# Moving a step's piece of attention ahead of its item of weight preparation in a two-layer fp32 block

## The chip, the core and the metric

The kernel runs on one core of one Trainium2 chip. The metric is the device time of one execution in microseconds (us). An execution of the kernel before takes 744.51 us, the median of three runs (743.21, 744.51 and 744.68).

## What is computed

The reference is a block of two equal layers. Sixteen learned meta tokens are put ahead of 512 input tokens, so T = 528, with a model width D of 1024, all in fp32. One layer does this:

```
h    = rms_norm(x, norm_gain)
proj = h @ w_in                      # q, k, v, gate_a, u_b, gate_b, q_idx, k_idx, w_idx, merge
q, k = rope(rms_norm(q)), rope(rms_norm(k));  q_idx, k_idx = rope(q_idx), rope(k_idx)
score[t, s] = sum over 8 heads of relu(q_idx . k_idx) * w_idx      # indexer
sel  = top 128 keys by score, in key chunks of 64 up to the query's own
attn = softmax(q . k over sel) @ v            # 8 heads of 64, one shared k and v
y_a  = (attn * silu(gate_a)) @ w_branch_a
y_b  = (pooled(u_b) * silu(gate_b)) @ w_branch_b
g_a, g_b = split(sigmoid(merge))              # 1024 columns each
x    = x + (g_a * y_a + g_b * y_b) @ w_out
```

The result is x after the two layers, without the meta tokens' rows.

## The kernel before

**Engines and orders.** TensorE (PE) and VectorE (DVE) run in the order in which the program issues their instructions (L101, a manual schedule for these two). ScalarE (ACT), GpSimd (POOL) and the DMA queue of SyncE (SP) are ordered by a scheduler, from the program's dependencies and from marks that the program sets. `Metered` (L52) adds up an estimated time for each instruction issued on PE and DVE; the program uses these sums to decide how much top-k selection it lets out.

**fp32 by halves.** A product of fp32 matrices is made of three matmuls on a faster type: high by high, low of the activations by high of the weights, high by low. For every weight there is a high part, a cast on ACT (L269), and a low part, a subtract on DVE of the high part from the raw weight. In the profile both are tiles named `w`, and DVE's instructions all carry line L63, that of the recording helper.

**Weight preparation.** Each chunk of 256 columns of `w_in` is multiplied by a scheme with seven products in place of eight, with the operands a11, a12, s2, s1, s3, s4 and a22. `mixed_prep` splits what a chunk needs into nine items, i0 to i8. An item is a few instructions: a cast of the next operand (`hi`), the subtract of the one before (`lo`), in some a sum on DVE (`s`, `raw<-s,raw`) and a DMA on POOL that adds one raw half to another (L255, L284). The last, i8, also issues the load of a later chunk on SP. The items wait in a queue, `prep_q`; `prep_one` takes the next. There are four raw buffers and eight `w` buffers.

**Groups of products.** `group_of_products` issues seven products of twelve matmuls each. `end()` follows every product: it calls `group_done`, and then takes further items until the chunk is as far ahead as `LEAD` (5 items) and the number of products done ask for. Copies of PSUM banks, `p` and `u` (ACT, L1019), and sums of a bank with such a copy, `c<-d,p` or `sila<-d,p` (DVE), set a bank free for a later product. `mix_gates` runs ten groups a layer; gates are tanh on ACT (L1059, L1065, L1069) and a multiply on DVE (`zb`, `sila`).

**Pieces of attention.** In `mix_gates` the attention is let out beside the products. Its generator makes three pieces a unit (a pair of heads of one block of 128 queries, sixteen units a layer): first the logits of the next unit on PE with the scaling of this one (reciprocal `rs` on DVE, `lt<-lt,rs` at L805 on ACT or on DVE, `pm` at L806 on POOL or DVE); then the softmax of the next unit (`lt<-a,sc` and `mn` on DVE, two exponentials at L791 on ACT) and the values of earlier ones on PE; then transposes on PE and their copies `pt` and `ptm` (ACT, L821 and L839), and the gated result `sila<-v,sila` (DVE). For the last four units the softmax comes with the first piece. `half_done` adds half of `rate` to a credit and lets out as many pieces as it has whole ones; `rate` is 1.4 and later 2.2 in the first layer, 1.6 in the second (L31). In the stage of the indexer, before these, `half_done` lets out indexer steps in the same way. An exponential is marked to be issued after the last copy of `p` or `u`.

**A step.** `group_done` does, in this order: instructions that became due (`later`), one item of preparation while `hold` allows one, `half_done`, and top-k selection as far as the metered time of PE leaves over.

Of the kernel before, what the change touches and what calls it, by code (L numbers as in the profile page):

```python
# [91 lines left out]
def tile_block(ctx: ExitStack, tc: tile.TileContext, x, meta, w_in, pool_w, w_a, w_b, w_out, rows, hgain, c_tab, out):  # L92
# [76 lines left out]
    def prep_one():  # L169
        popped[0] += 1  # L170
        prep_q.popleft()()
# [175 lines left out]
    def pump(n=1):  # L347
        for _ in range(n):
            while fill:
                try:  # L350
                    next(fill[0])
                    break
                except StopIteration:
                    fill.popleft()
# [6 lines left out]
    def half_done():  # L361
        credit[0] += rate[0] / 2
        n = int(credit[0])
        credit[0] -= n
        pump(n)

    def group_done():
        count[0] += 1
        due = [p for p in pend if p[0] <= count[0]]
        for p in due:  # L370
            pend.remove(p)
        for p in due:
            p[1]()
        if prep_q and hold[0]:
            hold[0] -= 1
            prep_one()
        half_done()
        spare[0] += share[0] * (pe.us - seen[0]) - (dve.us - seen[1])
        spare[0] = min(spare[0], CAP)
        seen[0], seen[1] = pe.us, dve.us  # L380
        while spare[0] > 0 and sel:
            before = dve.us
            try:
                next(sel[0])
            except StopIteration:
                sel.popleft()
            spare[0] -= dve.us - before
        seen[1] = dve.us
# [603 lines left out]
    def group_of_products(r, base, n2, operands, total, direct, mid=None):  # L992
# [18 lines left out]
        def end():  # L1011
            done[0] += 1
            group_done()
            while prep_q and (popped[0] < base + 9 * r + LEAD + done[0] * 9 // 7 or (mid and done[0] > 4)):
                prep_one()
# [202 lines left out]
    for l in range(2):  # L1218
# [20 lines left out]
        for t in (1, 2):  # L1239
            later(lambda t=t, ps=pss[t]: kv_post(l, t, ps), 1)  # L1240
        later(lambda ps=pss[0]: meta_sum(ps, KV, lambda total: kv_post(l, 0, total)), 1)
        group_done()
        for what, t in (("q", 1), ("q", 2), ("k", 3), ("k", 4), ("q", 3), ("q", 4)):
            if what == "k":
                ps = plain_group(t, raws[kv])
                later(lambda t=t, ps=ps: kv_post(l, t, ps), 1)
            else:
                index_queries(t, 0, w, hooks[1] if (l, t) == (1, 1) else None)
                if (l, t) == (0, 1):
                    ends.append(norm_half(0, 1, rstd, LAG1))  # L1250
            group_done()
            if (what, t) == ("k", 3):
                w_prep_enqueue(True, None if l else ends[0])
            if (what, t) == ("k", 4):
                del raws[kv]
                w_load()
# [318 lines left out]
```

## Time and profile before

| | us |
|---|---|
| median of the three runs | 744.51 |
| the profiled execution's own time | 744.49 |
| its span, first to last instruction | 742.7 |
| PE busy | 732.6 (99%) |
| weight loads of PE busy | 705.6 (95%) |
| DVE busy | 590.9 (80%) |
| ACT busy | 482.4 (65%) |
| POOL busy | 242.8 (33%) |

The granted clock of TensorE is 1.000. The merged-gate stages, in which attention runs beside the products, lie at about 172 to 310 us (first layer) and 538 to 664 us (second layer). A line of the timeline gives the start in us, the duration, the engine and line, the operation, the output and the inputs by the program's names, shapes, a count, and in brackets how long the engine had idled before and what released it. Lines of the waits view give the engine, what it was about to do, whom it waited for, and the total, the number and the longest of these waits.

### The profile page before, as it was taken

To read this page: it belongs to the slowest core of one execution; us is meant where nothing else is said; L and a number is where in the kernel's file an instruction comes from. 1 tells how busy PE (TensorE), PEld (TensorE's weight loads), DVE (VectorE), ACT (ScalarE), POOL (GpSimd) and SP (SyncE) were. 2 spreads that over 40 slices of the span, in tenths; PEclk is the share of its full clock that TensorE was granted. 3 is DMA by queue.
4 is the path that set the end of the run, shared out by engine and by line. 5 is a ranking of instruction groups with operands and counts; after the bars stand their busy time and mean duration, and the time that the engine had idled before them with its cause. 6 is when DMAs were issued, how large, how long until landed. Compare 5 with 4: busy or idle time off the path is not lost.

```text
span 742.7 us, 16105 instructions
## 1 busy us (share of the span) xinstructions
PE 732.6 (99%) x5949; PEld 705.6 (95%) x5949; DVE 590.9 (80%) x1500; ACT 482.4 (65%) x1099; POOL 242.8 (33%) x320
## 2 busy tenths in 40 slices
PE   8999999999999999999999999999999999999998
PEld 7999999899999999999999989998899999999997
DVE  6876899999897875894449668999989978768874
ACT  6669735656778886543236696367478977865643
POOL 3652173721221310063347410756021222105300
PEclk9999999999999999999999999999999999999999
DMA  8766774864564533543422677659464653448832
GB/s 265 231 154 165 166 158 114 214 158 100 119 139 114 123 64 101 173 156 117 143 88 86 170 171 198 157 128 204 109 156 100 147 111 86 116 107 261 201 89 72
DMA packets 103567, 106.42 MB, mean 143 GB/s; under 512 B 5008, under 2 KB 83632, under 8 KB 103488
## 3 DMA queue, kind: packets, MB, share of 16 engines
q1 hardware_dynamic: 91888, 74.89, 33.4%
q0 software_dynamic: 11520, 30.41, 22.8%
q8 instruction: 47, 0.77, 0.4%
q14 instruction: 32, 0.26, 0.1%
q10 hardware_dynamic: 80, 0.08, 0.0%
HBM read 66.41 MB, written 8.55 MB: 101 GB/s over the span
## 4 chain that ended last, share of the span: by engine, by line
PE 65%; DVE 23%; ACT 5%; issue 2%; DMA 2%; POOL 2%; SPq 1%; DVEq 0%; POOLq 0%; ACTq 0%
PE d L63 52%; PE a L63 9%; DVE sc L63 6%; DVE m L63 4%; PE v L63 4%; DVE w L63 2%; DVE t L63 2%; DMA xt<-in_x_dram 2%; ACT lt L791 1%; DVE lt L63 1%; DVE silb L63 1%; DVE us L63 1%; DVE mlo L63 1%; ACT w L225 1%; DVE qs L63 1%
## 5 line engine op out<-in xcount | busy, mean ns | idle before, releaser
L63 PE MATMUL d<-hhi,w 128*128 128x256 f32 (+3 forms) x1392 | 278.6, 291 | 0.8 <-DVE c L63 0.7
L63 PEld LDWEIGHTS d<-hhi,w 128*128 128x128 f32 x1392 | 222.4, 188 | 3.9 <-DVE c L63 1.2
L63 PE MATMUL d<-hlo,w 128*128 128x256 f32 (+3 forms) x696 | 189.9, 289 | 0.0
L63 DVE TENSOR_TENSOR w<-raw,w 128x512 fp32r<-128x512 f32 (+1 forms) x156 | 121.7, 786 | 20.7 <-ACT w L269 20.3
L63 PEld LDWEIGHTS d<-hlo,w 128*128 128x128 f32 x696 | 131.3, 189 | 1.4 <-issue 0.2
L63 PE MATMUL d<-hsum,w 128*128 128x264 f32 (+1 forms) x720 | 95.9, 285 | 0.6 <-ACT u L1019 0.3
L63 PEld LDWEIGHTS d<-hsum,w 128*128 128x128 f32 x720 | 89.6, 188 | 1.7 <-ACT u L1019 0.8
L63 PE MATMUL d<-w,hhi 128*128 128x256 f32 x576 | 86.1, 287 | 0.7 <-ACT sq L668 0.7
L269 ACT CAST w<-raw 128x512 fp32r<-128x512 f32 x132 | 78.7, 621 | 3.3 <-DMA raw<-s 1.4
L63 PEld LDWEIGHTS d<-w,hhi 128*128 128x128 f32 x576 | 74.7, 188 | 5.2 <-issue 2.3
L255 POOL DMA_DIRECT2D raw<-raw x22 | 19.8, 902 | 114.6 <-DMA raw<-in_w_in_dram 42.8
L221 POOL DMA_DIRECT2D w<-raw x34 | 31.5, 943 | 73.8 <-ACT w L220 51.1
L63 DVE MATCH_REPLACE8 sc<-m,sc 128x400 f32<-128x400 f32 (+2 forms) x100 | 54.5, 549 | 0.0
L791 ACT ACTIVATE lt<-lt,mn,NR 128x144 f32<-128x144 f32 (+3 forms) x64 | 42.2, 661 | 18.2 <-DVE mn L63 18.0
L63 DVE MAX8 m<-sc 128x8 f32<-128x400 f32 (+2 forms) x100 | 53.2, 557 | 0.9
L284 POOL DMA_DIRECT2D raw<-s x22 | 19.3, 879 | 91.0 <-DVE s L63 32.7
L63 DVE SCALAR_TENSOR_TENSOR sc<-r,wsg,sc 128x144 f32<-128x144 f32 (+3 forms) x56 | 32.4, 582 | 17.3 <-ACT r L714 15.0
L63 PE MATMUL d<-w,hlo 128*128 128x256 f32 x288 | 45.5, 281 | 0.0
L63 PE MATMUL d<-mhi,w 128*128 128x272 f32 (+2 forms) x192 | 45.2, 324 | 0.0
L677 POOL TENSOR_TENSOR t<-t,t 128x256 f32<-128x256 f32 (+1 forms) x34 | 32.5, 955 | 26.4 <-DVE t L63 25.0
L1420 POOL TENSOR_TENSOR hlo<-ta,hhi 128x256 fp32r<-128x256 f32 (+1 forms) x28 | 26.8, 966 | 43.6 <-PE d L63 31.4
L806 POOL TENSOR_SCALAR pm<-lt,rs 128x16 f32<-128x16 f32 x48 | 24.6, 573 | 47.3 <-DVE rs L63 47.3
(245 smaller groups left out, 1560.0 us busy)
## 6 DMA issues: line engine op xcount, KB each, us to landing
raw<-in_w_in_dram SPq DMA_DIRECT2D x88, 256.0 KB, 3.5
w<-raw POOLq DMA_DIRECT2D x34, 512.0 KB, 5.9
raw<-in_w_in_dram SPq DMA_DIRECT2D x32, 512.0 KB, 4.4
raw<-in_w_out_dram SPq DMA_DIRECT2D x12, 512.0 KB, 3.8
raw<-raw POOLq DMA_DIRECT2D x22, 256.0 KB, 4.2
raw<-s POOLq DMA_DIRECT2D x22, 256.0 KB, 3.3
kept<-res SPq DMA_DIRECT2D x16, 264.0 KB, 4.1
res<-kept SPq DMA_DIRECT2D x16, 264.0 KB, 6.4
```

Of the source, the lines that this page charges most:

```text
L63: return fn(*a, **k)
L221: gp.dma_start(t, raws[c][s], accum_op=OP.add)
L225: act.copy(t, raws[c][s])
L255: gp.dma_start(raws[c][0][:, 1], raws[c][0][:, 0], accum_op=OP.add)
L269: act.copy(t[:, 0], blk[src[n]])
L284: gp.dma_start(blk["a12"], blk["s2"], accum_op=OP.add)
L677: added[0] = gp.tensor_tensor(t1[:m, :256], t1[:m, :256], t2[:m, :256], op=OP.add).ins
L791: act.activation(L[hh][:, :n], L[hh][:, :n], AF.Exp, scale=NR[:, i, h:h + 1], bias=mn[:, hh:hh + 1], accum_out=sm[:, hh:hh + 1])
L806: (gp if j < 3 else dve).tensor_scalar(pms[i][:, 2 * j + hh, :], L[hh][:, 0:16], rs[:, hh:hh + 1], None, op0=OP.mult)
L1420: pool_end = gp.tensor_sub(hlo[:, j, a:a + n], d, f(hhi[:, j, a:a + n]))
```

## The change

In `group_done` the call of `half_done` goes ahead of the item of preparation. So in each step the piece of attention (or indexer step), if the credit lets one out, is issued before the item, and the item after it. Top-k selection still comes last, and no other line is changed.

```diff
         for p in due:
             p[1]()
+        half_done()
         if prep_q and hold[0]:
             hold[0] -= 1
             prep_one()
-        half_done()
         spare[0] += share[0] * (pe.us - seen[0]) - (dve.us - seen[1])
         spare[0] = min(spare[0], CAP)
```

The items that `end()` takes after `group_done` stay where they were, and so do those that a product takes because it needs them at once.

## The prediction

> **What bounds the kernel now.** I read the page first: the busy rows and the chain that ended last.
>
> ```profile
> PE 732.6 (99%) x5949; PEld 705.6 (95%) x5949; DVE 590.9 (80%) x1500; ACT 482.4 (65%) x1099; POOL 242.8 (33%) x320
> PE 65%; DVE 23%; ACT 5%; issue 2%; DMA 2%; POOL 2%; SPq 1%; DVEq 0%; POOLq 0%; ACTq 0%
> ```
>
> TensorE (PE) is busy 99% of the span and has the same matmuls in the same order after the change. The time can fall only by PE's waits and rise only by new ones. Attention and preparation of weights share the group steps where the orders of the two builds differ, and those are the two stages of merged gates. I split each into a tight half and a loose half by the windows view (us; then PE, PEld, DVE, ACT, POOL busy with counts; clock; DMA share; GB/s).
>
> ```profile
> 172.00:212.00 40.00, 39.26 (x326) 38.72 (x326) 36.35 (x103) 30.82 (x84) 7.84 (x14) 1.00 0.53 119
> 212.00:310.00 98.00, 97.84 (x869) 95.08 (x866) 74.79 (x204) 76.16 (x182) 17.12 (x27) 1.00 0.45 107
> 538.00:600.00 62.00, 61.56 (x534) 60.20 (x533) 56.41 (x163) 52.11 (x137) 16.05 (x24) 1.00 0.56 128
> 600.00:664.00 64.00, 63.84 (x587) 62.27 (x587) 45.22 (x123) 48.87 (x113) 11.77 (x17) 1.00 0.44 104
> ```
>
> In 172 to 212 and 538 to 600 VectorE (DVE) is busy 91% and ScalarE (ACT) 77 to 84% of the time, so a queue position there counts; later DVE falls to 71 to 76%. The waits view of PE's weight loads gives the ceiling, first of layer 0 (172 to 310), then of layer 1 (538 to 664); the second fence has DVE's waits for the casts, a row for each stage (total, times, longest).
>
> ```profile
> PEld d L63 <- DVE c L63: 1.2, 2, 1.0
> PEld d L63 <- ACT p L1019: 0.3, 1, 0.3
> PEld a L63 <- ACT lt L805: 0.2, 1, 0.2
> ...
> PEld d L63 <- ACT u L1019: 0.8, 2, 0.5
> PEld a L63 <- ACT lt L805: 0.5, 3, 0.2
> PEld a L63 <- DVE lt L63: 0.4, 1, 0.4
> PEld d L63 <- DVE w L63: 0.2, 1, 0.2
> ```
>
> ```profile
> DVE w L63 <- ACT w L269: 7.8, 9, 2.4
> DVE w L63 <- ACT w L269: 12.2, 12, 2.0
> ```
>
> These waits add up to 1.7 us in layer 0 and 1.9 us in layer 1: 3.6 us in all. More than that the change cannot win by removing waits that the trace names.
>
> **The change, part by part.** Nothing is added and nothing removed. Per step one item of preparation (a cast on ACT, a subtract "low" on DVE, sometimes a sum or a DMA) goes behind one piece of attention. In the built order PE is identical, DVE differs in 554 lines, ACT in 365, POOL in 72, SP in 10; all the differences lie in the two merged stages. The budget of the top-k selection sees the same amount of DVE work, since both pieces still precede it. What one place is worth on DVE is the low:
>
> ```profile
> L63 DVE TENSOR_TENSOR w<-raw,w 128x512 fp32r<-128x512 f32 x57 | 39.0, 686 | 11.6 <-ACT w L269 11.4
> ```
>
> A piece moved ahead of one low comes 0.69 us sooner; a low pays with the piece's length, 0.16 us for a reciprocal, 0.74 for the smallest softmax lead (144 columns, 198.37 to 199.11 below), more for wider ones.
>
> *Gain 1, layer 0, at 204.57.* DVE, ACT and PE rows of the timeline:
>
> ```profile
> 197.77 0.69 DVE L63 TENSOR_TENSOR w<-raw,w 128x512 fp32r<-128x512 f32 x1
> 198.37 0.31 DVE L63 CUSTOM_DVE_ANT_0 lt<-a,sc 128x144 f32<-128x144 f32 x1
> 198.95 0.16 DVE L63 TENSOR_TENSOR mn<-mn,RQ 128x2 f32<-128x2 f32 x1
> 199.20 0.51 ACT L791 ACTIVATE lt<-lt,mn,NR 128x144 f32<-128x144 f32 x1 [1.78 <-DVE mn L63]
> 201.44 0.43 DVE L63 SCALAR_TENSOR_TENSOR zb<-c,zb 128x264 f32<-128x264 f32 x1 [0.84 <-ACT c L1065]
> 203.55 0.28 PE L63 MATMUL d<-hhi,w 128*128 128x264 f32 x1
> 204.10 0.41 DVE L63 TENSOR_TENSOR c<-d,p 128x264 f32<-128x264 f32 x1
> 204.57 0.39 PE L63 MATMUL d<-hhi,w 128*128 128x264 f32 x1 [0.74 <-DVE c L63]
> ```
>
> PE waits for the total that frees its bank. The chain back is total, zb (0.84 us of DVE idle), the tanh behind two exponentials on ACT, and these wait 1.78 us for mn. In the new order mn stands ahead of the low of 197.77, 0.69 us sooner, and the tanh also passes a cast; zb's idle time goes, and the total comes about 0.8 sooner. PE lost 204.57 - 203.55 less one spacing of 0.12 = 0.9 there. I take 0.8 (ends 0.6 and 0.9). Next late there is DVE itself.
>
> *Gain 2, layer 1, at 540.57.* The same with a bank copy:
>
> ```profile
> 538.98 0.16 DVE L63 TENSOR_TENSOR mn<-mn,RQ 128x2 f32<-128x2 f32 x1
> 539.17 0.51 ACT L791 ACTIVATE lt<-lt,mn,NR 128x144 f32<-128x144 f32 x1 [1.58 <-DVE mn L63]
> 540.17 0.35 ACT L1019 COPY u<-d 128x256 f32<-128x256 f32 x1
> 538.32 1.94 PE L63 MATMUL d<-hsum,w 128*128 128x256 f32 x15
> 540.57 0.63 PE L63 MATMUL d<-hsum,w 128*128 128x256 f32 x3 [0.31 <-ACT u L1019]
> ```
>
> The 15 matmuls are 0.119 apart, so the next was due at 540.10: 0.47 lost, since the copy starts only as the second exponential ends. With mn 0.69 sooner all 0.5 goes (ends 0.3 and 0.5).
>
> *Smaller gains*, each bounded by its row of the first waits fence and by nothing: the copy of p in layer 0 (0.3; its exponentials follow a softmax lead that now passes a low), scaled rows L805 (0.2 and 0.5, of which I take 0.2 and 0.4, because reciprocals go ahead of low and sum), and lt scaled on DVE in layer 1 (0.4, likewise). Gains together: 0.8 + 0.5 + 0.3 + 0.2 + 0.4 + 0.4 = 2.6 us. The second wait for u and the "DVE w" row I leave standing (0.5 us).
>
> *Give-back 1, layer 1, at 557.* A cast goes behind exponentials:
>
> ```profile
> 551.50 0.61 ACT L269 CAST w<-raw 128x512 fp32r<-128x512 f32 x1
> 552.01 0.51 ACT L791 ACTIVATE lt<-lt,mn,NR 128x144 f32<-128x144 f32 x1
> 552.15 0.69 DVE L63 TENSOR_TENSOR w<-raw,w 128x512 fp32r<-128x512 f32 x1 [0.88 <-ACT w L269]
> 555.92 0.69 DVE L63 TENSOR_TENSOR w<-raw,w 128x512 fp32r<-128x512 f32 x1
> 557.28 0.40 PE L63 MATMUL d<-hhi,w 128*128 128x256 f32 x2
> ```
>
> DVE, already waiting for that cast, waits two exponentials longer: 2 x 0.505 = 1.01 (551.50 and 552.01 swap places). Nothing makes it up before the low of 555.92, which also has a reciprocal (0.16) put before it. That low ends at 556.60; the third matmul of its product, at 557.28, is the first to use it, and a release takes about 0.05 (204.51 to 204.57 above), so 0.63 covers it: 1.01 + 0.16 - 0.63 = 0.54 lost. Ends: 0, if the gain before it carries over in full, and 1.2, if PE comes there sooner and DVE doesn't. By the Trainium skill ("ScalarE: Activation LUTs", What ACT_TABLE_LOAD costs) an ACTIVATE with a pointer as bias takes about 280 ns + 0.833 ns a column, 0.40 us at 144, and consecutive ones overlap by 0.09; two of them would then delay the cast by some 0.6, and this term would fall to 0.15 as an estimate, the sum to about -1.6. The trace has 0.51 from start to start, each with an accumulator read, and the trace decides.
>
> *Give-backs 2 to 5.* The copy of p at 208.17 gets two exponentials ahead of it:
>
> ```profile
> 208.17 0.38 ACT L1019 COPY p<-d 128x264 f32<-128x264 f32 x1
> 208.96 0.62 ACT L791 ACTIVATE lt<-lt,mn,NR 128x272 f32<-128x272 f32 x1
> 209.86 0.41 PE L63 MATMUL d<-hsum,w 128*128 128x264 f32 x2
> ```
>
> It moves by 2 x 0.61 = 1.22, ending at 208.55 + 1.22 = 209.77 against PE's 209.86: between 0 and 0.8, if PE arrives by gain 1 earlier and the copy doesn't. I take 0.2. Three lows (one early in layer 0's loose half, two in layer 1's tight half) pay a softmax lead or a gated product ahead of them, and are ready for PE with about as much to spare; I put each between 0 and the 0.54 of give-back 1, and take 0.2. Together 0.8.
>
> *What costs nothing.* In the loose halves lows move back by a reciprocal, a scaled row and a whole lead of 528 columns, about four times 0.74 = 3.0 us. There the weight is ready long before use:
>
> ```profile
> 633.76 0.69 DVE L63 TENSOR_TENSOR w<-raw,w 128x512 fp32r<-128x512 f32 x1 [1.37 <-ACT w L269]
> 639.00 0.40 PE L63 MATMUL d<-hhi,w 128*128 128x256 f32 x2
> ```
>
> That low ends at 634.45, its first use is the third matmul of a product, at 639.00: 4.5 us, of which 1.5 stay; where less is left, PE would pay the difference, under 1 us. On POOL a few meta products (L806) pass the DMAs that add raw halves, and the load on SP follows a low that is later, by at most that 3.0. DVE's two stages show no wait for these DMAs, so I count nothing; without that cover the late piece costs up to 3 us once. On SP a load of the residual passes two of w_out, which are used in the stage after: nothing.
>
> *Sum.* -2.6 + 0.54 + 0.8 = -1.26 us. The profiled execution took 744.49 (span 742.7, 1.8 around it), as good as the median 744.51. 744.49 - 1.26 = 743.2.
>
> **The rivals.**
> (a) *The gains without the give-backs*: the ring of DVE and ACT starts earlier and stays earlier, so no low is late: 744.49 - 2.6 = 741.9. For it: both large waits stand at the beginning of their stage. Against: the lows move back by design at every step. All 3.6 us gone would give 740.9.
> (b) *No change*: DVE is 91% busy in the tight halves, and what PE stops waiting for is replaced by the next low: gains 1.3, give-backs 1.3: 744.5.
> (c) *Slower: casts behind exponentials.* By the built orders sixteen casts in 172 to 212 and 538 to 590 go behind one or two exponentials (0.5 to 0.6 us each), and DVE waits for casts 21 times already (the two rows above, 20.0 us). If three more places lose 0.54 as at 557 and the gains halve, 744.49 - 1.3 + 1.34 + 3 x 0.54 = 746.2; with no gain left, 747.5. It decides once the give-backs pass 2.6 + 1.5 = 4.1 us at full gains, or 2.8 at half. Against it: before the change PE waits only 0.2 us for a low in the whole of layer 1's stage. The Trainium skill ("PSUM — Partial Sum Buffer", Engine vs sequencer instructions) speaks for it: it calls ACT's and DVE's queues strictly first in, first out, so nothing passes a waiting exponential. The trace agrees where the copy of u starts at 540.17, as the exponential of 539.17 and its twin end.
>
> **How the numbers follow.** Forecast 0.38, (a) 0.17, (b) 0.13, (c) 0.32. About 0.2% (1.5 us, below 743.0 or above 746.0) is what a measurement of this kernel tells from no change. The forecast's own range is 742.2 to 744.2, by the ends of its terms: half of it counts as faster. With (a) faster is 0.19 + 0.17 = 0.36; same has the rest of the forecast, (b) and the lowest part of (c), 0.19 + 0.13 + 0.03 = 0.35; slower the rest of (c), 0.29. The range reaches to (a) below and past the middle of (c) above: 741.6 to 746.9.
>
> **What the profile after would show.** Right: PE's wait for c at about 204 and for u at about 540 gone, exponentials' waits for mn shorter in the tight halves; DVE's waits for casts grown in 538 to 600, one PE wait for a low or a hole of about 0.5 near 557, the loose halves unchanged within 0.3 us. Wrong: several new PE waits for w or p in the tight halves (c), a DVE wait for a sum or load, or PE's waits for c and u still there, because ACT orders the tanh and copies otherwise than I read them.

## The result

The changed kernel takes 740.65 us (median of 6 runs, 740.39 to 742.35). The kernel before, run beside it, took 743.75 us over all its 6 runs (743.02 to 744.68), 0.76 us less than the median shown ahead of the prediction. The ratio is 0.9964 with a 95% interval of 0.9953 to 0.9974, so it is faster, by 3.1 us between the medians and by 0.36% by the ratio. The prediction of 743.2 us (741.6 to 746.9) missed it. Rival (a), 741.9 us with gains and no give-backs, came nearest.

The page of the profile after has this busy row, then the chain:

```profile
PE 731.2 (99%) x5949; PEld 705.3 (95%) x5949; DVE 590.0 (80%) x1500; ACT 483.1 (65%) x1099; POOL 246.1 (33%) x320
PE 75%; DVE 17%; ACT 2%; DMA 2%; issue 2%; POOL 1%; SPq 1%; DVEq 0%; POOLq 0%; ACTq 0%
```

The engines are busy for as long as before, within 4 us each; PE's share of the chain rose from 65% to 75%, those of DVE and ACT fell. The windows view of the four halves, with the columns of the prediction's:

```profile
172.00:212.00 40.00, 39.93 (x335) 39.39 (x335) 37.43 (x108) 31.69 (x85) 8.82 (x14) 1.00 0.57 132
212.00:310.00 98.00, 97.97 (x865) 95.31 (x863) 74.48 (x200) 76.24 (x180) 18.03 (x27) 1.00 0.46 109
538.00:600.00 62.00, 61.95 (x543) 61.13 (x542) 56.23 (x159) 52.60 (x137) 18.92 (x26) 1.00 0.58 133
600.00:664.00 64.00, 64.00 (x591) 62.78 (x590) 46.01 (x123) 49.13 (x112) 9.93 (x15) 1.00 0.44 106
```

In the first tight half PE did 335 matmuls in 40 us where it did 326. The waits of its weight loads that are left, of the kinds that the prediction counted (layer 0 from 172 to 310 first, then layer 1 from 538 to 664), and DVE's waits for casts in the two:

```profile
PEld d L63 <- ACT p L1019: 0.3, 1, 0.3
PEld a L63 <- ACT lt L805: 0.2, 1, 0.2
PEld d L63 <- DVE c L63: 0.2, 1, 0.2
...
PEld d L63 <- DVE w L63: 0.3, 1, 0.3
```

```profile
DVE w L63 <- ACT w L269: 6.4, 8, 1.2
DVE w L63 <- ACT w L269: 5.5, 5, 2.2
```

Of the 3.6 us that bounded the gain, 1.0 is left. DVE waits less for casts, 11.9 us in place of 20.0. This goes with the place of the low behind a piece of attention, which leaves the cast more time: in the two runs below that cut the item in two, these waits are 24.3 us with the lows ahead and 9.2 us with the casts ahead.

PE's order is the same in both builds, so each matmul can be matched with itself in the other trace. The shift is the start of a matmul after less its start before. This table gives the steps of the shift, from before a place to behind it: a minus is a gain of the changed kernel, a plus a loss. Places are times of the before trace, and steps under 0.12 us are left out.

| place, us | what PE waited for | step, us | the prediction's term |
|---|---|---|---|
| 19.6 | the input's load (not of the change) | -1.12 | none |
| 184 | scaled lt | -0.22 | smaller gains, -0.2 |
| 204.6 | c | -0.95 | gain 1, -0.8 |
| 209.9 | p | +0.33 | give-back 2, +0.2 |
| 237 | scaled lt | +0.23 | none |
| 288 | p | -0.43 | smaller gains, -0.3 |
| 540.6 | u | -0.58 | gain 2, -0.5 |
| 545.6, 545.9 | scaled lt | -0.43 | smaller gains, -0.4 |
| 557.3 | a low | +0.32 | give-back 1, +0.54 |
| 577.5 | u | -0.38 | left standing, 0 |
| 655.3, 655.5 | lt scaled on DVE | -0.55 | smaller gains, -0.4 |

A wait costs more than itself. In the stages the matmuls of a product stand 0.12 us apart. At 204.57, 288.10, 540.57 and 577.54, and in the trace after at 207.84 and 554.26, the matmul behind the one that waited stands 0.22 or 0.23 us behind it. So with each such wait another 0.1 us comes or goes, and the waits view doesn't count it.

From behind the input's wait to the end, the shift grows from -1.07 to -3.87: 2.8 us come from the change, 3.5 of gains less 0.9 of losses in the table, and the rest in small steps. The rest of the difference of the two spans (742.7 and 738.8) is one wait at the start of the profiled execution of before:

```profile
19.59 0.87 PE L63 MATMUL a<-consts,xt 128*128 128x128 f32 x6 [1.21 <-DMA xt<-in_x_dram]
```

The profile after has no such wait, and of the twelve variants below only two have it (1.0 and 1.4 us), so it belongs to single executions, as far as these profiles show, and not to the change.

The place of gain 1 in the trace after:

```profile
196.38 0.30 DVE L63 CUSTOM_DVE_ANT_0 lt<-a,sc 128x144 f32<-128x144 f32 x1
196.94 0.16 DVE L63 TENSOR_TENSOR mn<-mn,RQ 128x2 f32<-128x2 f32 x1
197.02 0.69 DVE L63 TENSOR_TENSOR w<-raw,w 128x512 fp32r<-128x512 f32 x1
197.20 0.51 ACT L791 ACTIVATE lt<-lt,mn,NR 128x144 f32<-128x144 f32 x1 [0.81 <-DVE mn L63]
199.19 0.43 DVE L63 SCALAR_TENSOR_TENSOR zb<-c,zb 128x264 f32<-128x264 f32 x1
201.85 0.41 DVE L63 TENSOR_TENSOR c<-d,p 128x264 f32<-128x264 f32 x1
202.24 0.47 PE L63 MATMUL d<-hhi,w 128*128 128x264 f32 x2
```

The low of 0.69 us stands behind mn, the first exponential waits 0.81 us in place of 1.78, zb no longer waits at all, and PE goes on without a wait behind the total.

### The profile page after: what moved, and what is told of

Its sections match the earlier page's. It is cut to its first block, busy times and chain, and to the rows that moved or that the text cites. A ratio compares the mean times of both kernels' runs of the same rounds, so it can differ in the third digit from the quotient of the medians.

```text
span 738.8 us, 16099 instructions
## 1 busy us (share of the span) xinstructions
PE 731.2 (99%) x5949; PEld 705.3 (95%) x5949; DVE 590.0 (80%) x1500; ACT 483.1 (65%) x1099; POOL 246.1 (33%) x320
## 4 chain that ended last, share of the span: by engine, by line
PE 75%; DVE 17%; ACT 2%; DMA 2%; issue 2%; POOL 1%; SPq 1%; DVEq 0%; POOLq 0%; ACTq 0%
PE d L63 60%; PE a L63 10%; DVE sc L63 5%; PE v L63 4%; DVE m L63 3%; DMA xt<-in_x_dram 2%; DVE t L63 1%; DVE w L63 1%; DVE nf L63 1%; DVE silb L63 1%; DVE us L63 1%; DVE mlo L63 1%; DMA raw<-s 1%; ACT w L225 0%; SPq L156 0%
## 5 line engine op out<-in xcount | busy, mean ns | idle before, releaser
L791 ACT ACTIVATE lt<-lt,mn,NR 128x144 f32<-128x144 f32 (+3 forms) x64 | 42.2, 661 | 12.1 <-DVE mn L63 12.0
L284 POOL DMA_DIRECT2D raw<-s x22 | 19.6, 892 | 90.6 <-DVE s L63 42.8
L806 POOL TENSOR_SCALAR pm<-lt,rs 128x16 f32<-128x16 f32 x48 | 27.9, 622 | 44.7 <-DVE rs L63 31.9
```

The lines of the kernel that those rows point to most:

```text
L284: gp.dma_start(blk["a12"], blk["s2"], accum_op=OP.add)
L791: act.activation(L[hh][:, :n], L[hh][:, :n], AF.Exp, scale=NR[:, i, h:h + 1], bias=mn[:, hh:hh + 1], accum_out=sm[:, hh:hh + 1])
L806: (gp if j < 3 else dve).tensor_scalar(pms[i][:, 2 * j + hh, :], L[hh][:, 0:16], rs[:, hh:hh + 1], None, op0=OP.mult)
```

## The experiments

All runs are set beside runs of the kernel before on the same chip; the kernel before had medians of 743.43 to 743.94 us there. Steps of the shift come from one profiled execution of each run. "Net of the stages" is the shift of PE against the trace of before, from behind the start to the end, so without the input's wait.

**One layer at a time.** The edit, for the first layer (for the second `at[0] == 1`); `at` is set to the layer where its attention begins:

```diff
-        half_done()
-        if prep_q and hold[0]:
-            hold[0] -= 1
-            prep_one()
+        early = at[0] == 0
+        if early: half_done()
+        if prep_q and hold[0]: hold[0] -= 1; prep_one()
+        if not early: half_done()
```

> Attention goes ahead of the item in the first layer only; the second layer steps as before. Theory A (the gain is the sum of a few PE waits that vanish one by one in each layer's merged stage; step by step the traces of before and after show about 1.0 us net in the first layer and 1.7 us net in the second): 743.75 - 1.0 = 742.7 us, PE's wait for c at about 204 us gone, no shift of PE added between 538 and 664. Theory B (the gain is of the program as a whole: the schedule or the start, where the two profiled executions already differ by 1.07 us before anything is changed): no clear gain or the whole 3.1 us, and no such place.

> Attention goes ahead of the item in the second layer only. Theory A: 743.75 - 1.7 = 742.0 us, PE's wait at about 204 us back with 0.9 us, the waits for u at 540 and for lt at 545 and 655 gone. Theory B: no clear gain, or as much as the whole change.

Measured: 741.96 us for the first layer alone (before 743.43; ratio 0.9978, 0.9968 to 0.9988), net of the stages -1.16 us; 741.88 us for the second alone (0.9982, 0.9972 to 0.9993), net -1.38. Each layer's waits go in its own stage and stay in the other's: 0.92 us at 204.6 in the one, 0.57 at 540.6, 0.41 at 545 and 0.54 at 655 in the other. The two gains, 1.5 and 1.6 us, add up to the whole. Theory A held, B fell.

**One kind of piece at a time.** With `early = at[1] >= 0` only softmax pieces go ahead, with `early = at[1] < 0` only the others; before each `yield`, the generator notes in `at[1]` the unit whose softmax the next piece holds, or -1:

```diff
-            yield
+            at[1] = u + 1 if u + 1 < 12 else -1; yield
             if u + 1 < 12:
                 soft(u + 1)
```

> Only the pieces that begin with a softmax lead go ahead of their item, in both layers; scaling, transposes and gated products stay behind. Theory A (an earlier mn, so earlier exponentials, so earlier copies and tanh behind them): the waits at 204, 288, 540 and 577 us go, about 2.3 us, and the give-backs of 0.2 us near 208 and 557 stay; the waits for lt at 545 and 655 us stay. Net -1.8: 742.0 us. Rival C (what counts is that every low is issued later, so that DVE waits less for casts): about half of 3.1 us here and half in the complement, spread over many steps.

> The complement: pieces without a softmax lead (scaling with its reciprocal, transposes, gated products) go ahead of their item, softmax pieces stay behind. Theory A: the waits for the scaled lt at 184, 545 and 655 us go, about 1.1 us; the waits at 204 and 540 us stay: 742.7 us. Rival C: about half of the whole gain, 742.2 us, with fewer DVE waits for casts everywhere.

Measured: softmax pieces alone 743.31 us (ratio 0.9997, 0.9985 to 1.0008), net -0.21; the others alone 742.98 us (0.9990, 0.9981 to 1.0000), net -0.60. The waits that theory A named went (0.68 us at 204.6 and 0.58 at 540.6 with the softmax pieces; those for lt with the others), yet together the halves make 0.6 us of 3.1. For the softmax pieces both totals fell, as 742.0 and about 742.2 us lie below the interval; for the others either theory's total lies within the interval. New waits took their place. With the others alone, PE comes sooner to a copy of u that still stands behind late exponentials, and loses 0.52 us there (ACT and PE rows of the timeline):

```profile
198.35 0.51 ACT L791 ACTIVATE lt<-lt,mn,NR 128x144 f32<-128x144 f32 x1 [1.80 <-DVE mn L63]
199.35 0.36 ACT L1019 COPY u<-d 128x264 f32<-128x264 f32 x1
199.76 1.23 PE L63 MATMUL d<-hsum,w 128*128 128x264 f32 x8 [0.32 <-ACT u L1019]
```

With softmax pieces alone, PE loses 0.77 us between 555 and 557, where the whole change loses 0.32, and 0.23 at 577, where it wins 0.38.

**Which kind lacks which.** Two more cuts: softmax pieces with the third pieces (gated product, transposes), and softmax pieces with the scaling pieces. They differ only in which kind of piece gets -2 in `at[1]`, under this condition:

```diff
+        early = at[1] >= -1
```

> Softmax pieces and the third pieces (gated product and transposes) go ahead of their item; scaling pieces without a softmax stay behind. With softmax pieces alone PE lost 0.35 us at about 576 us to a copy of u behind the gated product's cast and the scaled rows, where the whole change wins 0.29. Theory G (a late piece left behind becomes the next wait as soon as the wait ahead of it is gone, so the kinds do not add up): that place turns from +0.35 to a gain, the waits for the scaled lt at 545 and 655 us stay with 1.0 us together, total 742.5 us against 743.3 for softmax alone. Rival H (the missing gain is in the scaling pieces alone): no change against softmax alone, 743.3 us.

> Softmax pieces and scaling pieces go ahead of their item; only the third pieces (gated product and transposes) stay behind. Theory K (softmax and scaling need each other: an earlier mn brings PE and ACT forward, and then the next thing that ACT's queue stands still for is the reciprocal of the scaled rows ahead of a copy of u, unless that goes ahead too): nearly the whole gain, 740.7 to 741.3 us, the place at about 576 us no loss, the one near 557 us under 0.3. Rival L (the three kinds together are needed, each loses most without the others): 742.3 us or more.

Measured: with the third pieces 743.45 us (1.0002, 0.9992 to 1.0011), no better than softmax alone: theory G fell, rival H held, and the gated product was the wrong suspect. With the scaling pieces 741.09 us (0.9971, 0.9961 to 0.9981), net -2.4 of 2.8: theory K held, but for the place near 557, which loses 0.38 us where it said under 0.3. Against the gated-product run the place near 577 turns from a loss of 0.28 to a gain of 0.34. There the order of the reciprocal counts. Softmax with third pieces:

```profile
573.48 1.28 DVE L63 TENSOR_TENSOR w<-raw,w 128x512 fp32r<-128x512 f32 x2
574.68 0.16 DVE L63 RECIPROCAL rs<-sm 128x2 f32<-128x2 f32 x1
574.76 0.69 DVE L63 TENSOR_SCALAR sc<-sc 128x400 f32<-128x400 f32 x2
...
575.22 0.91 ACT L805 ACTIVATE lt<-lt,rs 128x256 f32<-128x256 f32 x2 [1.00 <-DVE sc L63]
576.03 0.35 ACT L1019 COPY u<-d 128x256 f32<-128x256 f32 x1
...
576.43 0.50 PE L63 MATMUL d<-hsum,w 128*128 128x256 f32 x2 [0.41 <-ACT u L1019]
```

The whole change:

```profile
571.83 0.68 DVE L63 TENSOR_TENSOR w<-raw,w 128x512 fp32r<-128x512 f32 x1
572.43 0.16 DVE L63 RECIPROCAL rs<-sm 128x2 f32<-128x2 f32 x1
572.50 0.67 DVE L63 TENSOR_TENSOR w<-raw,w 128x512 fp32r<-128x512 f32 x1
...
572.62 0.91 ACT L805 ACTIVATE lt<-lt,rs 128x256 f32<-128x256 f32 x2
573.43 0.35 ACT L1019 COPY u<-d 128x256 f32<-128x256 f32 x1
```

With the reciprocal behind two lows, ACT stands idle for 1.00 us ahead of the scaled rows, and behind those stands the copy that frees PE's bank. With the reciprocal between the lows, the rows start 0.03 us behind its end (572.59), and the copy is in time. The reciprocal's place is not the whole of the 1.00 us: the rows start 0.38 us behind its end (574.84), and the profile puts the wait down to `sc`, the multiply right behind it on DVE; why they wait for that long isn't shown. Scaling stands in front of copies as exponentials do; here, bringing forward the one alone left a stall at the other.

**One step.** The whole change, except that one softmax piece (unit 3 of the first layer, that of gain 1) goes behind its item: `early = at != [0, 3]`. On DVE this moves one low.

> The changed kernel, but the softmax piece of unit 3 in the first layer goes behind its item again: one low, that of 197.77 us before the change, stands ahead of one softmax lead. Theory A: PE's wait for c at about 202 us comes back with 0.8 to 0.95 us, nothing else moves: 740.65 + 0.9 = 741.5 us. Rival E (DVE's and ACT's ring makes up for one place, so single places mean little and only all of them together do): under 0.3 us.

Measured: 741.07 us (before 743.94; 0.9955, 0.9940 to 0.9970). The interval holds both theories, so the trace must tell. PE waits at the place of gain 1 again:

```profile
201.86 0.28 PE L63 MATMUL d<-hhi,w 128*128 128x264 f32 x1
202.54 0.39 PE L63 MATMUL d<-hhi,w 128*128 128x264 f32 x1 [0.40 <-DVE c L63]
```

Less a spacing of 0.12 that is 0.56 us lost, where the kernel before lost 0.90, and the step at this place is -0.35 us in place of -0.95. Of these 0.6 us, 0.33 are made up at once at 209.9, since p is then no longer late for PE. The net is 0.3 us against the whole change: theory A's return of 0.8 to 0.95 fell, and E's limit of 0.3 us is met in sum, not at the place itself. So some 0.6 of the 0.95 us came from that low; the rest, which goes with the pieces brought forward ahead of it, wasn't taken apart.

**Lows or casts.** Each item was cut in two, so that either its DVE part (and its DMAs) or its casts could stay ahead of the piece. Part 1 is the casts, part 2 the lows, sums and DMAs; the lines are of the run with lows ahead, and the other run has the numbers exchanged (cut: how an item is divided):

```diff
+            item.part(2)
+            half_done()
+            item.part(1)
```

> Each item is cut in two: its lows and sums on DVE (and its DMAs) stay ahead of the piece of attention, only its casts go behind. DVE's order is that of the kernel before. Theory A (DVE's place of mn, reciprocal and gated product carries the gain): no gain, 743.4 us, with the waits at 204 and 540 us there; at most 0.5 us slower by casts behind exponentials. Rival D (the gain is made on ACT, by tanh and copies that pass casts): half of it or more, 742.0 us or less.

> The other cut: the casts of the item are issued ahead of the piece of attention, lows, sums and DMAs behind it. DVE's order is that of the changed kernel but for three places. Theory A: the whole gain, 740.7 us, and the lost 0.2 us each near 208 and 557 us smaller or gone: 740.3 to 740.7. Rival D: the tanh behind its cast loses part of the gain at 204 us: 741.5 us or more.

Measured: lows ahead, casts behind 744.38 us (before 743.94; 1.0010, 0.9998 to 1.0021). PE keeps the wait at 540.6 and all but 0.16 us of that at 204.6, and loses 0.49 us at 179, 0.28 at 258, 0.27 at 557 and 0.37 at 623; net of the stages it loses 1.0 us in the trace, while the times aren't clear of no change. Casts ahead, lows behind 740.94 us (0.9963, 0.9949 to 0.9978), net -2.9: the whole gain, with no loss at 557 and 0.33 at 209.9. The place of the low on DVE carries the gain; casts that go behind the piece, without the lows, win nothing in sum. Theory A held. D fell with the lows ahead; in one place it has a share, as with casts ahead the gain at 204.6 is 0.70 us in place of 0.95: there the tanh stands behind a cast again. DVE's order is the same by kind of instruction in this run and the changed kernel, and in the run with lows ahead and the kernel before.

**How far ahead the preparation runs.**

```diff
-LEAD = 5
+LEAD = 6
```

and the same with 4.

> The changed kernel with the preparation one item further ahead of the products (LEAD 6 in place of 5). Theory A: what the change gives back is late lows, so the 0.15 to 0.4 us near 557 us go and nothing else changes: 740.4 us. Rival F: the further lead puts more lows ahead of softmax leads at other places, so waits of the first kind return: 741 us or more.

> The changed kernel with the preparation one item less ahead of the products (LEAD 4). LEAD 6 cost 8 us by totals on DVE that free a bank and stood behind more lows. Theory I (the order of lows against everything else on DVE decides, and 5 items is about the balance): weight pieces with under 1 us to spare come late at several places, 742 to 746 us. Rival J (the fewer lows ahead, the better, as in the change itself): 740 us or less.

Measured: LEAD 6 748.74 us (before 743.94; 1.0067, 1.0044 to 1.0089), LEAD 4 760.62 us (before 743.55; 1.0230, 1.0215 to 1.0245). Rival F (LEAD 6) and theory I (LEAD 4) held in their direction, J fell; the size of LEAD 4 is far past the 746 that I gave, and in LEAD 6 PE waits for totals rather than for the softmax. The two rows of waits for totals in LEAD 6 (from 168 to 312; from 536 to 664 those for c are 3.0 us), then LEAD 4's for lows in both:

```profile
PEld d L63 <- DVE sila L63: 2.1, 2, 1.3
PEld d L63 <- DVE c L63: 1.3, 2, 1.0
```

```profile
PEld d L63 <- DVE w L63: 6.8, 9, 1.8
PEld d L63 <- DVE w L63: 6.3, 6, 2.1
```

One item more ahead, and totals that free a bank come late; one item less, and the weights themselves are late. So the change isn't the same as letting out less preparation.

**One place earlier still.** The piece ahead of the instructions that became due:

```diff
+        half_done()
         for p in due:
             p[1]()
-        half_done()
```

> The changed kernel with the piece of attention let out one place earlier still, ahead of the instructions that became due in the step (gate multiplies, subtracts). These move by 0.4 us of DVE at most and are waited for by few. Theory A: the waits that are left in the merged stages are about 0.5 us in all, so at most 0.3 us is to be won, 740.4 to 741.0 us. Rival J (earlier attention is better everywhere): 740 us or less.

Measured: 741.57 us (before 743.55; 0.9971, 0.9962 to 0.9981). Not better than the change, and rival J falls; against theory A's 741.0 it is 0.6 us more, less than what the intervals tell apart. This edit does more than the theory said, as it also moves indexer steps: PE's order differs from that of the changed kernel at 40 to 90 and at 409 to 456 us. In the merged stages the trace gains 2.8 us, as the change does, but between 400 and 530 us it loses 1.3, where PE has a wait that the changed kernel doesn't have:

```profile
PE a L63 <- DVE us L63: 1.3, 1, 1.3
```

No version tried is clearly faster than the changed kernel.

## Why the prediction was wrong

The mechanism was right in the main: the two large waits went with the lows that moved, and the loss at 557 came. The step that failed is the sum, term by term: gains were taken at 2.6 us and came to 3.5, give-backs were taken at 1.34 and came to 0.9, and the base was 0.74 us too high.

- **The bound** held for the net, 2.8 of 3.6 us, in the two merged stages alone. It didn't hold for single terms, which the prediction limited by their rows: the copy of p gave 0.43 us for a row of 0.3, because the 0.1 us of the matmul behind a wait stands in no row.
- **Gains 1 and 2** were right in mechanism and nearly in size: 0.95 for 0.8, 0.58 for 0.5. The claim that one low of 0.69 us stands for gain 1 was right in part: undoing that one low brings 0.6 us back.
- **The smaller gains** were 0.22, 0.43, 0.43 and 0.55 us, 1.63 against 1.3. **The second wait for u**, put at nothing without a reason, gave 0.38 more: the reciprocal ahead of its copy's scaled rows passes a low, as shown at 577.
- **Give-back 1** was mis-sized: 0.54 forecast, 0.32 measured. Rows before, then after:

```profile
552.76 1.18 DVE L63 MAX8 m<-sc 128x8 f32<-128x400 f32 x2
554.04 0.42 DVE L63 TENSOR_TENSOR sila<-d,p 128x256 f32<-128x256 f32 x1
...
548.28 0.50 ACT L791 ACTIVATE lt<-lt,mn,NR 128x144 f32<-128x144 f32 x1
548.77 0.50 ACT L791 ACTIVATE lt<-lt,mn,NR 128x144 f32<-128x144 f32 x1
549.26 0.61 ACT L269 CAST w<-raw 128x512 fp32r<-128x512 f32 x1
549.90 0.69 DVE L63 TENSOR_TENSOR w<-raw,w 128x512 fp32r<-128x512 f32 x1 [1.40 <-ACT w L269]
550.51 1.18 DVE L63 MAX8 m<-sc 128x8 f32<-128x400 f32 x2
551.61 0.41 DVE L63 TENSOR_TENSOR sila<-d,p 128x256 f32<-128x256 f32 x1
553.53 0.68 DVE L63 TENSOR_TENSOR w<-raw,w 128x512 fp32r<-128x512 f32 x1
554.26 0.50 PE L63 MATMUL d<-hhi,w 128*128 128x256 f32 x2
```

PE's shift is -3.23 us as it comes here. Against that the cast is 0.99 us late (549.26 for 551.50) and the first low 0.98, as summed. The step "nothing makes it up" failed: the total behind the two maxima starts 1.10 us behind them in place of 1.28, so 0.18 is made up there, and the reciprocal takes 0.08 from its start to the next one (552.26 to 552.34), not 0.16. The low that PE needs is 0.84 us late where 1.17 were summed. With 0.63 of cover that is a wait of 0.21, and the matmul behind it adds 0.1. With the casts ahead of the exponentials nothing is lost here, so the order of the cast is the cause. The second layer alone, which has the change's orders of DVE and ACT in this layer, loses 0.53: ahead of the copy of u a cast waits 0.68 us for the DMA `raw<-s` in place of 0.43 (the DMA takes 0.26 us longer from its issue), so that the copy, the exponentials and the cast behind them are 0.2 us later still.

- **Give-backs 2 to 5**: the copy of p cost 0.33 for 0.2. Of the three lows taken at 0.2 each none shows.
- **The DMAs that add raw halves** were counted at nothing, because DVE shows no wait for them. The engine that waits is ACT, whose casts read them. Its rows before (538 to 664; from 172 to 310 it has none), then after (172 to 310, 538 to 664), and the place of the loss at 237:

```profile
ACT w L269 <- DMA raw<-s: 0.2, 1, 0.2
...
ACT w L269 <- DMA raw<-s: 2.1, 3, 1.1
ACT w L269 <- DMA raw<-s: 1.2, 3, 0.6
...
229.94 0.86 POOL L284 DMA_DIRECT2D raw<-s  x1 [2.31 <-ACT lt L791]
233.85 0.62 ACT L269 CAST w<-raw 128x512 fp32r<-128x512 f32 x1 [1.11 <-DMA raw<-s]
234.38 0.91 ACT L805 ACTIVATE lt<-lt,rs 128x256 f32<-128x256 f32 x2
```

The DMA is issued 0.92 us later against PE than before (230.93 with a shift of -1.91), as its sum stands behind a softmax lead. The cast waits for it, with the scaled rows behind it, and PE loses 0.23 us.

- **The sum** was then -1.26 where the traces show -2.8: 0.9 by gains, 0.5 by give-backs, 0.1 in steps under 0.12 us. (The medians show 3.1, which the interval doesn't tell from 2.8.) The base adds 0.74 us to the miss in the absolute time: the forecast began at 744.49 us, an execution with 1.21 us of waiting for its input, and the median of all six runs of the kernel before is 743.75.
- **Rival (c)**, slower by casts behind exponentials, shows by itself in the trace: casts behind the piece without the lows lose 1.0 us net, in four places. With the lows behind the piece too, one such place is left, that near 557. The sign that DVE's waits for casts would grow in 538 to 600 was wrong: they fell from 3.5 to 2.5 us. **Rival (b)** is what the times show when only one of the two kinds is moved.
- **The duration by the Trainium skill** ("ScalarE: Activation LUTs", What ACT_TABLE_LOAD costs) was worked out in the prediction for one pointer operand. The exponentials have two, bias and scale (L791), and the page adds about 93 ns for each. That makes 0.49 us at 144 columns as an estimate, and 0.40 with the overlap. The trace agrees with it: an exponential takes 0.50 us, and the accumulator's read starts 0.40 us behind its start (548.28 and 548.68). The read adds the rest of the 0.49 us from one exponential's start to the next. So the 0.15 us that the prediction worked out for the term at 557 rested on one pointer operand too few.

## What to carry to other kernels

Where several engines run in order and PE is the bound, put the short instruction that another engine stands still for (a minimum, a reciprocal) ahead of the long one whose result is needed later, and do so for every kind that shares a queue: with the exponentials or the scaled rows alone left late, 3.1 us became 0.5 or 0.1. When a wait is priced, add the slower matmul behind it. Look for the waits for a late DMA on the engine that reads it. Before a sum is taken from one profiled execution, look at its start for waits that don't belong to the kernel.

## What had not been expected

The pieces' kinds don't add up: 0.1 and 0.5 us apart, 3.1 us together, while the two layers do add up, 1.5 and 1.6. And one item of preparation more or less ahead makes the changed kernel 8 and 20 us slower, far more than the whole change moves.
